# Softmax times values in three fp32r products instead of one fp32 product

## The chip, the cores and the metric

The kernel runs on one core of a Trainium2 chip. The metric is the time of one launch on the device in microseconds (us), median of several runs. The engines are called PE (matrix products), ACT (scalar engine), DVE (vector engine), POOL (general engine) and SP (which issues most DMAs).

## What is computed

One inference step of an encoder with two layers, for 1024 frames of a new stream and 8 running streams of 16 frames each; all 1152 columns go through the same weights (model width 1024). Layer 0 is a mixer of a state-space model and a gated delta rule, then a gated feed-forward net. Layer 1 is attention in a sliding window with grouped heads, then a gated feed-forward net. The change is in the attention over the new stream:

```
q: 16 heads, k and v: 4 heads, head width 64, chunks of 64 frames
scores = einsum('bnqkgd,bnskd->bnkgqs', q, kband) / 8   # chunk n sees chunks n-2, n-1, n
p = softmax over s of [scores, sink][..., :-1]
o = einsum('bnkgqs,bnskd->bnqkgd', p, vband)            # this product is changed
out = o @ wo
```

Everything is fp32 in the reference.

## The kernel before

Matrices are kept with features on the 128 partitions and frames in the free dimension, in three blocks of 384 columns. The large products with weights are not done in fp32, but as three products in fp32r, a rounded form of fp32: a matrix is split in a rounded part (`hi`, made by an ACT copy into an fp32r tile) and a remainder (`lo`, made by a DVE subtraction), and hi·hi + hi·lo + lo·hi is summed in PSUM. `gemm_block` and `project` do that; their PSUM tile is called pg in the profile.

`swa` is the attention of layer 1. It projects keys and values (`gemm` with `wkv`); values are transposed on PE so that frames stand on partitions, and stored in one fp32 tile `vT` of nine 128-frame tiles by 256 columns (4 heads of 64). Then, for each of two pairs of key/value heads, `qgemm(pair)` projects the queries and `attend(pair)` runs 16 chunks. `prompt_unit` does one chunk for the two heads e = 0, 1 of the pair:

- the scores of the four query heads that share a key head, two matmuls into a PSUM tile pS (L1896);
- `soft`: maximum, exponential, sum, reciprocal and scaling on DVE, ACT and POOL, in one of three tiles `pt_` (L1871 to L1884);
- up to two 128-frame key tiles hold the window. For each, two transposes on PE (L1916) into a PSUM tile pT (two banks), then a DVE copy of all of them to SBUF (L1919, or L1921 where there is one key tile);
- the product with the values: per key tile one fp32 matmul (L1923). The stationary operand is `vT[lo:hi, t, 64 columns of this head]`, the moving one the 256 columns of transposed weights, and the result stands on the 64 PSUM partitions of this head in one tile pO.

After both heads, pO is stored in one operation: an ACT copy to `o0` for the first pair (L1977), and for the second pair directly as the rounded part and remainder that the output projection wants (L1988, L1989). After every second chunk `sample_unit` does one of the running streams in the same way, in fp32, through the same tile ring `sT`.

Each engine has its own queue, in an order that is fixed before the run by a planner: it simulates the engines with costs of its own and, among what is ready in that simulation, takes what stands earliest in the program (a block `Sooner` moves work up). So `attend(0)` has precedence over `qgemm(1)`, which stands behind it, and `attend(1)` over the first half of the output projection (`project`, L1543 to L1545), whose first input, the first pair's output, is complete at that time. These projections are what PE does while it would wait for a softmax. When `attend(1)` is over, `between` closes the attention's pools and frees their space for the second half of the output projection.

`ssq` is a fixed tile in a pool of the whole program, which holds sums of squares for the norms and serves as scratch elsewhere; the attention does not use it.

Of the kernel before, what the change touches and what calls it, by code (L numbers as in the profile page):

```python
# [25 lines left out]
TP = 1024  # L26
# [176 lines left out]
def body(tc, nc, I, O):  # L203
# [136 lines left out]

    ssq = rp.tile([128, T], F32, name="ssq")

    def square_in(x, k, b, i, new, parts, keep=None):

        s = blk(b)
        if i == 0:
            S.activation(ssq[:, s], x[:, k, s], AF.Square)
            parts[:] = [ssq[:, s]]  # L350
            return
        both = keep is not None
        sq = keep if both and i == 2 else new()
        S.activation(sq, x[:, k, s], AF.Square)
        if i == KC - 1 or both and i == 2:
            parts.append(sq)
        elif both and i % 2 == 0:
            V.tensor_add(parts[1], parts[1], sq)
        else:
            P.tensor_add(ssq[:, s], ssq[:, s], sq)  # L360

    def rms(r, b, parts, first=0, banks=None):


        s = blk(b)
        y, v = r[:, s], ssq[:, s]
# [95 lines left out]
    def ffn(x, pre, l, w, nxt):  # L462
# [221 lines left out]
        for n in "gu":  # L684
# [4 lines left out]
        nt = rp.tile([128, BW], F32, name="nt", tag="nt", bufs=1)  # L689
        rooms = [[tp.tile([128, BW], F32, name=f"sg{i}") for i in range(2)] + [ssq[:, blk(b)] for b in range(NB)] + [nt] +  # L690
                 [r[:, blk(UP_T[t])] for t in (0, 2)],
# [78 lines left out]
        nt, rr = rp.tile([128, BW], F32, name="nt", tag="nt", bufs=1), new_r()  # L770
        sums = [nt, rr[:, blk(0)], ssq[:, blk(0)], ssq[:, blk(1)]] + sums + [ssq[:, blk(2)], rr[:, blk(1)], rr[:, blk(2)]]
        seven = {(n, m): sums[4 * i + m] for i, n in enumerate(("B11", "T2", "T3")) for m in range(4)}
# [282 lines left out]
    P.tensor_copy(PW[:, :, 0], L8)  # L1055
    tp = ssq[:, 0:256].rearrange("p (n q g) -> p n q g", q=2, g=16)
    for n in (1, 2, 4, 8):
# [30 lines left out]
    XG = XE[:, 0:TP // CS].rearrange("p (a c) q g -> p a c q g", c=16)  # L1088
    sc = ssq.rearrange("p (u v g) -> p u v g", v=2, g=16)
    for c in range(1, 16):  # L1090
# [200 lines left out]
    for hh in range(1, H):  # L1291
        gate_in(hh, ssq)

# [47 lines left out]
    def gate(t):  # L1341
        zs = h4(ssq[:, blk(t % 2, 512)])
        Q.dma_start(zs, d_z[:, :, blk(t, 128)].rearrange("h p i -> p h i"))
        return zs
# [465 lines left out]
def swa(env):  # L1810
# [6 lines left out]
    kT = qp.tile([128, 2, T], F32, name="kT")  # L1817
    vT = qp.tile([128, NT, 256], F32, name="vT")
    qt = [p_.tile([128, 4 * T], F32, name=f"q{i}") for i, p_ in enumerate((q0p, qp))]
# [7 lines left out]
    for t in (snk, snks):  # L1827
        V.tensor_scalar(t[:, 1], t[:, 0], -1.0, None, op0=ALU.mult)
    wk, c_wk = po.open("swv")

    W = [panel(I["wkv"][m]) for m in range(2)]
# [4 lines left out]
    for m in range(2):  # L1836
        def ev(b, s, p):
# [8 lines left out]
    Q.dma_start(O["pv"], vT[:, 7, :])  # L1846
# [4 lines left out]
    Q.dma_start(O["sv"][:, 112:128, :], vT[:, 8, :])  # L1851
    d_vn = env["dr"].tile([128, 256], F32, name="d_vn")
    Q.dma_start(d_vn, vT[:, 8, :])

# [9 lines left out]
    def small(n, w=2):  # L1864
        return wk.tile([128, w], F32, name=n, tag=n, bufs=4)

# [18 lines left out]

    def prompt_unit(pair, c, out):
        pO = mbank("pO")
        for e in range(2):
# [35 lines left out]
        out(c, pO[:, :256].rearrange("p (i k) -> p i k", i=4))  # L1924

    ns = npt

    def sample_unit(pair, b, out, ck, cvt, vn):
# [9 lines left out]
        pT = mbank("pT")  # L1938
        sT = wk.tile([128, 2, 2, 128], F32, name="sT", tag="sT", bufs=2)
        for i in range(2):  # L1940
            PE.transpose(pT[:, i * 128:i * 128 + 128], pt[:, 0, 64 + 128 * i:192 + 128 * i], ident)
        V.tensor_copy(sT[:, 0].rearrange("p a k -> p (a k)"), pT[:, :256])
        pO = mbank("pO")
        for e in range(2):
            hs = slice(64 * e, 64 * e + 64)
            PE.matmul(pO[hs, :64], cvt[:, b, hs], sT[:, 0, 0, hs], start=True, stop=False)
            PE.matmul(pO[hs, :64], vn[:, b, hs], sT[0:16, 0, 1, hs], start=False, stop=True)
        out(b, pO[:, :64].rearrange("p (i k) -> p i k", i=4))

# [11 lines left out]
    def attend(pair, store, then=lambda: None):  # L1961
# [5 lines left out]
        Q.dma_start(cvt, I["cv"][:, :, 128 * pair:128 * pair + 128].rearrange("b t c -> t b c"))  # L1967
        then()
        for c in range(16):
            prompt_unit(pair, c, lambda c, p: store(c, slice(0, 64), p))  # L1970
            if c % 2:
                continue
            b = c // 2
            sample_unit(pair, b, lambda b, p: store(16 + b // 4, slice(LS * (b % 4), LS * (b % 4) + LS), p), ck, cvt, vn)

    qgemm(0)
    attend(0, lambda c, k, src: S.copy(o0[:, c, :, k], src))  # L1977
    qgemm(1)
# [6 lines left out]

    def store1(c, k, src):
        oh, ol = (t[:, c % 6, :, k] for t in oT[c // 6][1])
        S.copy(oh, src)  # L1988
# [5 lines left out]

    def between():
        c_wk()
        c_qp()
# [15 lines left out]
```

## Time and profile before

| what | value |
|---|---|
| median of 3 runs | 2709.62 us (2709.35 to 2715.86) |
| profiled execution, its own time | 2709.62 us |
| its span, first to last instruction | 2707.8 us |
| mean granted TensorE clock | 0.973 |
| PE busy | 2556.9 us, 94% of the span |
| DVE, POOL, ACT busy | 1979.3, 1625.4, 1146.3 us |
| the two calls of `attend` | about 1550 to 1850 us |

The profile is one execution, recorded instruction by instruction. An fp32 matmul appears as two records on PE, an fp32r matmul as one (both are printed as f32). PEld is the load of the stationary operand. The recorded duration of a matmul runs from its start to its modelled end, and matmuls overlap in the pipeline: what one costs is read from the distance of the starts, or from the chain that ended last. The granted clock is a share of 2.4 GHz; 0.50 is 1.2 GHz.

### The profile page before, as it was taken

The page shows a single profiled execution, that of the slowest core. Times are in us where ns is not written, and L with a number is a line of the kernel's source. Part 1 is how long each engine was busy: PE and PEld are TensorE (multiplying, and loading weights), DVE is VectorE, ACT ScalarE, POOL GpSimd, SP SyncE. Part 2 cuts the span into 40 slices and gives each one's busy share as a digit, 9 for nine tenths or more (in the row PEclk, how much of TensorE's full clock was granted, in tenths as well). Part 3 has the DMA queues.
Part 4 walks back from the last instruction along what each step waited for, and adds up shares of the span by engine and source line. Part 5 has one row for each costly group of instructions (what it writes and reads, how often), then busy time and mean ns, then how long its engine had stood idle before and what let it go on. Part 6 is the DMA issues. An engine that isn't in the chain of part 4 may idle for free.

```text
span 2707.8 us, 40377 instructions
## 1 busy us (share of the span) xinstructions
PE 2556.9 (94%) x14777; PEld 2382.5 (88%) x14777; DVE 1979.3 (73%) x3235; ACT 1146.3 (42%) x2312; POOL 1625.4 (60%) x1659
## 2 busy tenths in 40 slices
PE   6898899999799999989999999999889999989996
PEld 5787798999799999989998977677889999989996
DVE  7847874567878777798866245555878777788967
ACT  5234465345544444443333134434544444444333
POOL 8749532125698888887532022213589888888735
PEclk9899999999999999999999999998999999999998
DMA  6432377633122222253213200202122222243311
GB/s 208 126 114 77 102 237 230 190 121 111 37 101 79 91 74 74 93 185 100 93 38 106 69 16 19 93 30 86 43 98 82 86 76 74 76 177 119 96 49 70
DMA packets 164166, 267.21 MB, mean 99 GB/s; under 512 B 34188, under 2 KB 123948, under 8 KB 162928
## 3 DMA queue, kind: packets, MB, share of 16 engines
q1 hardware_dynamic: 163392, 262.28, 29.9%
q8 instruction: 116, 1.90, 0.3%
q10 hardware_dynamic: 576, 2.36, 0.2%
q14 instruction: 82, 0.67, 0.1%
HBM read 186.92 MB, written 79.51 MB: 98 GB/s over the span
## 4 chain that ended last, share of the span: by engine, by line
PE 68%; POOL 11%; DVE 11%; DMA 4%; issue 4%; ACT 1%; SPq 1%; DVEq 0%; POOLq 0%; ACTq 0%
PE pa L455 7%; PE pa L454 7%; PE pa L453 7%; PE pd L455 3%; PE pd L453 3%; PE pd L454 3%; PE b L453 3%; PE b L455 3%; PE b L454 3%; PE pg L320 3%; PE pg L322 3%; PE pg L321 3%; PE pO L1923 2%; PE pg L1543 2%; PE pg L1544 2%
## 5 line engine op out<-in xcount | busy, mean ns | idle before, releaser
L453 PE MATMUL pa<-u,whi 128*128 128x384 f32 x904 | 307.4, 341 | 20.6 <-ACT whi L535 10.9
L454 PE MATMUL pa<-u,whi 128*128 128x384 f32 x904 | 306.3, 339 | 1.1 <-DVE u L269 1.1
L455 PE MATMUL pa<-u,wlo 128*128 128x384 f32 x904 | 298.1, 338 | 6.3 <-DVE wlo L536 6.3
L535 ACT CAST whi<-x 128x1024 fp32r<-128x1024 f32 (+2 forms) x184 | 132.5, 747 | 257.1 <-PE pa L454 172.1
L454 PE MATMUL pd<-g,whi 128*128 128x384 f32 x708 | 240.2, 339 | 0.0
L453 PE MATMUL pd<-g,whi 128*128 128x384 f32 x708 | 239.3, 338 | 0.0
L455 PE MATMUL pd<-g,wlo 128*128 128x384 f32 x708 | 237.8, 338 | 0.4 <-DVE wlo L298 0.4
L536 DVE TENSOR_TENSOR wlo<-x,whi 128x1024 fp32r<-128x1024 f32 (+2 forms) x184 | 213.0, 1180 | 24.7 <-ACT whi L535 24.4
L1884 POOL TENSOR_SCALAR p<-p,rd 128x192 f32<-128x192 f32 (+3 forms) x80 | 60.0, 752 | 278.4 <-DVE rd L1878 157.3
L453 PEld LDWEIGHTS pa<-u,whi 128*128 128x128 f32 x904 | 171.5, 190 | 25.5 <-ACT whi L535 14.5
L297 ACT CAST whi<-raw 128x1024 fp32r<-128x1024 f32 x113 | 116.6, 1049 | 173.7 <-PE pg L321 81.6
L531 POOL TENSOR_TENSOR x<-x 128x256 f32<-128x256 f32 (+1 forms) x186 | 169.4, 931 | 24.9 <-DVE wlo L536 18.8
L531 POOL TENSOR_TENSOR x<-raw 128x256 f32<-128x256 f32 (+1 forms) x186 | 169.4, 933 | 21.5 <-DVE wlo L536 13.3
L298 DVE TENSOR_TENSOR wlo<-raw,whi 128x1024 fp32r<-128x1024 f32 x113 | 165.3, 1465 | 22.7 <-ACT whi L297 20.3
L455 PEld LDWEIGHTS pa<-u,wlo 128*128 128x128 f32 x904 | 170.8, 190 | 7.7 <-DVE wlo L536 7.6
L531 POOL TENSOR_TENSOR cm<-raw 128x256 f32<-128x256 f32 (+1 forms) x150 | 144.3, 983 | 49.8 <-DVE wlo L536 18.5
L454 PEld LDWEIGHTS pa<-u,whi 128*128 128x128 f32 x904 | 171.8, 190 | 2.3 <-DVE u L269 1.9
L453 PE MATMUL pa<-u,x 128*128 128x384 f32 x428 | 145.8, 341 | 5.3 <-ACT x L535 2.8
L320 PE MATMUL pg<-h0h,whi 128*128 128x384 f32 x384 | 135.4, 353 | 12.1 <-DVE ut L970 11.4
L454 PE MATMUL pa<-u,x 128*128 128x384 f32 x428 | 144.9, 338 | 0.0
L455 PE MATMUL pa<-u,x 128*128 128x384 f32 x428 | 141.6, 339 | 0.0
L790 DVE TENSOR_TENSOR g<-gf,g 128x384 fp32r<-128x384 f32 x132 | 137.4, 1066 | 5.3 <-ACT g L789 5.3
(735 smaller groups left out, 8113.7 us busy)
## 6 DMA issues: line engine op xcount, KB each, us to landing
gf<-d_g SPq DMA_DIRECT2D x44, 576.0 KB
raw<-in_wd_dram SPq DMA_DIRECT2D x44, 512.0 KB
raw<-in_wg_dram SPq DMA_DIRECT2D x24, 512.0 KB
raw<-in_wu_dram SPq DMA_DIRECT2D x24, 512.0 KB
raw<-in_win_dram SPq DMA_DIRECT2D x21, 512.0 KB
x<-in_wg_dram SPq DMA_DIRECT2D x20, 512.0 KB
x<-in_wu_dram SPq DMA_DIRECT2D x20, 512.0 KB
d_r<-x SPq DMA_DIRECT2D x24, 384.0 KB
```

The source lines that it names most:

```text
L297: S.copy(hi, raw)
L298: V.tensor_sub(lo, raw, hi)
L320: PE.matmul(p[:, :BW], hi[:, c], rh, start=(i == 0), stop=False)
L321: PE.matmul(p[:, :BW], hi[:, c], rl, start=False, stop=False)
L322: PE.matmul(p[:, :BW], lo[:, c], rh, start=False, stop=(i == len(ks) - 1))
L453: PE.matmul(p, hi[:, c], uh, start=start, stop=False, skip_group_check=more)
L454: PE.matmul(p, hi[:, c], ul, start=False, stop=False, skip_group_check=more)
L455: PE.matmul(p, lo[:, c], uh, start=False, stop=stop, skip_group_check=more)
L531: (P.tensor_add if sg > 0 else P.tensor_sub)(cm[:, 256 * j:256 * (j + n)], fa, ga)
L535: S.copy(hi[:, c], src)
L536: V.tensor_sub(lo[:, c], src, hi[:, c])
L790: eng.tensor_sub(op[1], t, op[0])
```

## The change

Four things change, all for the product of the prompt chunks; `sample_unit` keeps its fp32 product.

1. The values are stored by pairs of heads, eight tiles of 128 frames by 128 columns, as a rounded part `vh` and a remainder `vl`. Those of the first pair are made when the values are transposed; the second pair's are kept in fp32 (`v1`) and split at the start of `attend(1)` by `values`, into the same buffers. `vl` lives in the buffer of `ssq`, which therefore becomes a tile that is made anew after the attention.
2. The transposed weights are rounded by an ACT copy out of PSUM (`sh`), and DVE subtracts that from PSUM for the remainder (`sl`); before, one DVE copy took them out.
3. Per key tile there are three fp32r matmuls with a stationary operand of 128 by 128 (both heads of the pair) and 256 moving columns; of the result only the 64 partitions of the head in question are used. Its two heads stand side by side in pO, 256 columns each.
4. The output is stored in two operations of 64 partitions, one for each head.

Beside that the ring of the small softmax vectors goes from 4 to 3 buffers, and the two value tiles that go out as results have a tile of their own.

```diff
+    V0 = halves()
+    v1 = qp.tile([128, NV, 128], F32, name="v1")
...
-            S.copy(vT[:, 3 * b:3 * b + 3, 128 * m:128 * m + 128], pt[:, :BW].rearrange("p (t i) -> p t i", t=3))
+            p3 = pt[:, :BW].rearrange("p (t i) -> p t i", t=3)
+            t = slice(3 * b, min(3 * b + 3, NV))
+            p2 = p3[:, :t.stop - t.start]
+            S.copy((v1 if m else V0[0])[:, t], p2)
+            if not m:
+                V.tensor_sub(V0[1][:, t], p2, V0[0][:, t])
+            if b == NB - 1:
+                S.copy(vT[:, :, 128 * m:128 * m + 128], p3[:, 1:])
...
-        return wk.tile([128, w], F32, name=n, tag=n, bufs=4)
+        return wk.tile([128, w], F32, name=n, tag=n, bufs=3)
...
+    def values(pair):
+        if not pair:
+            return V0
+        vh, vl = halves()
+        S.copy(vh, v1)
+        V.tensor_sub(vl, v1, vh)
+        return vh, vl
...
-            sT = wk.tile([128, 2, 2, 128], F32, name="sT", tag="sT", bufs=2)
+            sh, sl = (wk.tile([128, 512], F32R, name=n, tag=n, bufs=2) for n in ("sh", "sl"))
...
-            if nk == 2:
-                V.tensor_copy(sT.rearrange("p i a k -> p (i a k)"), pT)
-            else:
-                V.tensor_copy(sT[:, 0].rearrange("p a k -> p (a k)"), pT[:, :256])
-            for i, (t, w, lo, hi) in enumerate(ks):
-                PE.matmul(pO[hs, :256], vT[lo:hi, t, 64 * kv:64 * kv + 64], sT[lo:hi, i].rearrange("p a k -> p (a k)"), start=(i == 0), stop=(i == nk - 1))
-        out(c, pO[:, :256].rearrange("p (i k) -> p i k", i=4))
+            for o in (sh, sl):
+                a, b = o[:, :256 * nk], pT[:, :256 * nk]
+                S.copy(a, b) if o is sh else V.tensor_sub(a, b, sh[:, :256 * nk])
+
+            terms = [(x_, y[:, blk(i, 256)], t) for i, (t, *_) in enumerate(ks) for x_, y in ((v[0], sh), (v[0], sl), (v[1], sh))]
+            for i, (x_, y, t) in enumerate(terms):
+                PE.matmul(pO[:, blk(e, 256)], x_[:, t], y, start=(i == 0), stop=(i == len(terms) - 1))
+        for e in range(2):
+            hs = slice(64 * e, 64 * e + 64)
+            out(c, hs, pO[hs, blk(e, 256)].rearrange("p (i k) -> p i k", i=4))
...
+        v = values(pair)
         for c in range(16):
-            prompt_unit(pair, c, lambda c, p: store(c, slice(0, 64), p))
+            prompt_unit(pair, c, lambda c, hs, p: store(c, hs, slice(0, 64), p), v)
```

## Rows read from the trace of the kernel before

**Rows 1.** The page, part 1: busy time, share of the span, instructions.

```profile
PE 2556.9 (94%) x14777; PEld 2382.5 (88%) x14777; DVE 1979.3 (73%) x3235; ACT 1146.3 (42%) x2312; POOL 1625.4 (60%) x1659
```

**Rows 2.** Windows: stretch, its length, busy us (records) by engine, clock, DMA.

```profile
1450.00:1500.00 50.00, 50.00 (x288) 48.64 (x287) 17.78 (x32) 9.17 (x15) 0.46 (x1) 1.00 0.23 69
...
1675.00:1703.00 28.00, 27.89 (x159) 17.22 (x158) 17.25 (x63) 14.71 (x57) 6.68 (x9) 1.00 0.24 72
...
sum 300.00, PE 296.84 PEld 204.05 DVE 161.56 ACT 125.94 POOL 59.98; mean PE 59.37 PEld 40.81 DVE 32.31 ACT 25.19 POOL 12.00
```

**Rows 3.** The chain that ended last, 1550 to 1850 us, shares by line.

```profile
by line: PE pO L1923 22.4%; PE pS L1896 17.4%; PE pT L1916 10.6%; PE pg L320 6.5%; PE pg L322 6.4%; PE pg L1543 6.1%; PE pg L321 6.1%; PE pg L1545 5.8%; PE pg L1544 5.7%; PE pO L1946 2.8%; PE pO L1947 2.7%; PE pS L1933 2.2%; PE pT L1941 1.9
```

**Rows 4.** Windows of the tile pg alone: length, PE, PEld, DVE, ACT, clock, DMA.

```profile
1550.00:1675.00 125.00, 63.76 (x289) 48.75 (x289) 6.93 (x16) 0.00 (x0) 1.00 0.06 18
1675.00:1703.00 28.00, 5.19 (x26) 3.94 (x24) 0.62 (x2) 0.00 (x0) 1.00 0.24 72
1703.00:1716.00 13.00, 0.00 (x0) 0.00 (x0) 1.01 (x2) 0.00 (x0) 0.82 0.88 339
```

**Rows 5.** Windows of 4 us: PE, PEld, DVE, ACT, POOL, clock, DMA.

```profile
1714.00:1718.00 4.00, 4.00 (x12) 2.48 (x11) 2.41 (x9) 1.39 (x6) 0.60 (x1) 0.50 0.18 75
...
1844.00:1848.00 4.00, 3.15 (x8) 1.24 (x8) 0.76 (x2) 1.92 (x3) 0.41 (x1) 0.55 0.00 0
```

**Rows 6.** Windows of line L1923 alone: length, PE, PEld, clock, DMA.

```profile
1550.00:1675.00 125.00, 25.67 (x84) 7.96 (x84) 1.00 0.06 18
1675.00:1703.00 28.00, 9.76 (x35) 3.11 (x36) 1.00 0.24 72
1703.00:1716.00 13.00, 3.93 (x10) 0.97 (x10) 0.82 0.88 339
```

**Rows 7.** Timeline of PE: start, duration, line, operation, tiles, records.

```profile
1587.48 1.09 PE L1916 MATMUL pT<-ident,p 128*128 128x128 f32 x8
1588.33 0.42 PE L320 MATMUL pg<-h0h,whi 128*128 128x384 f32 x1
...
1604.09 0.44 PE L320 MATMUL pg<-h1h,whi 128*128 128x384 f32 x1
1604.37 0.34 PE L321 MATMUL pg<-h1l,whi 128*128 128x384 f32 x1
1604.54 0.35 PE L322 MATMUL pg<-h1h,wlo 128*128 128x384 f32 x1
```

**Rows 8.** Timeline of PE at half clock.

```profile
1717.72 0.52 PE L1544 MATMUL pg<-o0l,whi 128*128 128x384 f32 x1
1718.04 0.52 PE L1545 MATMUL pg<-o0h,wlo 128*128 128x384 f32 x1
```

**Rows 9.** Groups by form: busy us, mean ns, idle before and its releaser.

```profile
L1919 DVE COPY sT<-pT 128x512 f32<-128x512 f32 x56 | 38.6, 690 | 29.4 <-PE pT L1916 28.5
L1500 ACT COPY o<-pO 128x512 f32<-128x512 f32 x8 | 4.7, 585 | 15.3 <-PE pO L1499 15.3
L1359 DVE TENSOR_TENSOR pn<-pn,sq 128x512 f32<-128x512 f32 x9 | 6.3, 698 | 0.2
L1977 ACT COPY o<-pO 128x256 f32<-128x256 f32 x16 | 6.0, 373 | 30.3 <-PE pO L1923 30.3
L297 ACT CAST whi<-raw 128x1024 fp32r<-128x1024 f32 x11 | 11.4, 1043 | 14.1 <-PE pg L321 12.1 <-PE pg L1544 1.9
L298 DVE TENSOR_TENSOR wlo<-raw,whi 128x1024 fp32r<-128x1024 f32 x11 | 14.1, 1291 | 2.3 <-PE pO L1923 2.3
```

**Rows 10.** The chain that ended last, in order: start, length, what.

```profile
1827.26 1.15 PE pO L1923 x4
...
1830.67 0.84 PE pS L1896 x4
...
1844.28 2.10 PE pO L1923 x4
```

**Rows 11.** Waits in 1550 to 1850: in total, times, longest.

```profile
PE pO L1923 <- DVE sT L1919: 1.6, 2, 0.8
```

More of the change, by code (lines that the diff above doesn't have):

```diff
@@ L339, in split_in, with new_ssq @@
         V.scalar_tensor_tensor(h[b][k][1], x[:, k, blk(b)], wk, h[b][k][0], ALU.mult, ALU.subtract)
-    ssq = rp.tile([128, T], F32, name="ssq")
+    SS = []
+    def new_ssq():
+        SS[:] = [rp.tile([128, T], F32, name="ssq", tag="ssq", bufs=1)]
+    new_ssq()
     def square_in(x, k, b, i, new, parts, keep=None):
@@ L348, in square_in @@
         if i == 0:
-            S.activation(ssq[:, s], x[:, k, s], AF.Square)
-            parts[:] = [ssq[:, s]]
+            S.activation(SS[0][:, s], x[:, k, s], AF.Square)
+            parts[:] = [SS[0][:, s]]
             return
@@ L359, in square_in @@
         else:
-            P.tensor_add(ssq[:, s], ssq[:, s], sq)
+            P.tensor_add(SS[0][:, s], SS[0][:, s], sq)
     def rms(r, b, parts, first=0, banks=None):
         s = blk(b)
-        y, v = r[:, s], ssq[:, s]
+        y, v = r[:, s], SS[0][:, s]
         t = rp.tile([128, BW], F32, name="nt", tag="nt", bufs=1)
@@ L689, in ffn @@
         nt = rp.tile([128, BW], F32, name="nt", tag="nt", bufs=1)
-        rooms = [[tp.tile([128, BW], F32, name=f"sg{i}") for i in range(2)] + [ssq[:, blk(b)] for b in range(NB)] + [nt] +
+        rooms = [[tp.tile([128, BW], F32, name=f"sg{i}") for i in range(2)] + [SS[0][:, blk(b)] for b in range(NB)] + [nt] +
                  [r[:, blk(UP_T[t])] for t in (0, 2)],
@@ L770, in ffn @@
         nt, rr = rp.tile([128, BW], F32, name="nt", tag="nt", bufs=1), new_r()
-        sums = [nt, rr[:, blk(0)], ssq[:, blk(0)], ssq[:, blk(1)]] + sums + [ssq[:, blk(2)], rr[:, blk(1)], rr[:, blk(2)]]
+        sums = [nt, rr[:, blk(0)], SS[0][:, blk(0)], SS[0][:, blk(1)]] + sums + [SS[0][:, blk(2)], rr[:, blk(1)], rr[:, blk(2)]]
         seven = {(n, m): sums[4 * i + m] for i, n in enumerate(("B11", "T2", "T3")) for m in range(4)}
@@ L1055, in body @@
     P.tensor_copy(PW[:, :, 0], L8)
-    tp = ssq[:, 0:256].rearrange("p (n q g) -> p n q g", q=2, g=16)
+    tp = SS[0][:, 0:256].rearrange("p (n q g) -> p n q g", q=2, g=16)
     for n in (1, 2, 4, 8):
@@ L1088, in body @@
     XG = XE[:, 0:TP // CS].rearrange("p (a c) q g -> p a c q g", c=16)
-    sc = ssq.rearrange("p (u v g) -> p u v g", v=2, g=16)
+    sc = SS[0].rearrange("p (u v g) -> p u v g", v=2, g=16)
     for c in range(1, 16):
@@ L1291, in body @@
     for hh in range(1, H):
-        gate_in(hh, ssq)
+        gate_in(hh, SS[0])
     mphase(pX=1, pU=1, pc=1, pO=1, sm=1, m=1)
@@ L1341, in gate @@
     def gate(t):
-        zs = h4(ssq[:, blk(t % 2, 512)])
+        zs = h4(SS[0][:, blk(t % 2, 512)])
         Q.dma_start(zs, d_z[:, :, blk(t, 128)].rearrange("h p i -> p h i"))
@@ L1817, in swa, with halves @@
     kT = qp.tile([128, 2, T], F32, name="kT")
-    vT = qp.tile([128, NT, 256], F32, name="vT")
+    NV = TP // 128
+    def halves():
+        return (qp.tile([128, NV, 128], F32R, name="vh", tag="vh", bufs=1),
+                env["rp"].tile([128, T], F32, name="vl", tag="ssq", bufs=1)[:, :TP].bitcast(F32R).rearrange("p (t i) -> p t i", t=NV))
+    V0 = halves()
+    v1 = qp.tile([128, NV, 128], F32, name="v1")
     qt = [p_.tile([128, 4 * T], F32, name=f"q{i}") for i, p_ in enumerate((q0p, qp))]
@@ L1829, in swa @@
     wk, c_wk = po.open("swv")
+    vT = wk.tile([128, 2, 256], F32, name="vT")
     W = [panel(I["wkv"][m]) for m in range(2)]
@@ L1842, in ev @@
                 PE.transpose(pt[:, blk(t, 128)], vv[:, blk(t, 128)], ident)
[L1843 removed]
+            p3 = pt[:, :BW].rearrange("p (t i) -> p t i", t=3)
[6 more added lines that the diff above has]
+                S.copy(vT[:, :, 128 * m:128 * m + 128], p3[:, 1:])
         gemm(panel(I["wkv"][2 + m]), h, ev)
     Q.dma_start(O["pk"].rearrange("m p t -> p m t"), kT[:, :, TP - 128:TP])
[L1846 removed]
+    Q.dma_start(O["pv"], vT[:, 0, :])
     for m in range(2):
@@ L1850, in swa @@
     Q.dma_start(O["sv"][:, 0:112, :], I["cv"][:, 16:128, :])
-    Q.dma_start(O["sv"][:, 112:128, :], vT[:, 8, :])
+    Q.dma_start(O["sv"][:, 112:128, :], vT[:, 1, :])
     d_vn = env["dr"].tile([128, 256], F32, name="d_vn")
-    Q.dma_start(d_vn, vT[:, 8, :])
+    Q.dma_start(d_vn, vT[:, 1, :])
     c_wk()
@@ L1884, in soft, with prompt_unit @@
                 P.tensor_scalar(q, q, rd[:, a:a + 1], None, op0=ALU.mult)
-    def prompt_unit(pair, c, out):
+    def values(pair):
[5 more added lines that the diff above has]
+        return vh, vl
+    def prompt_unit(pair, c, out, v):
         pO = mbank("pO")
@@ L1938, in sample_unit @@
         pT = mbank("pT")
-        sT = wk.tile([128, 2, 2, 128], F32, name="sT", tag="sT", bufs=2)
+        sT = wk.tile([128, 2, 128], F32, name="sT", tag="sT", bufs=1)
         for i in range(2):
             PE.transpose(pT[:, i * 128:i * 128 + 128], pt[:, 0, 64 + 128 * i:192 + 128 * i], ident)
-        V.tensor_copy(sT[:, 0].rearrange("p a k -> p (a k)"), pT[:, :256])
+        V.tensor_copy(sT.rearrange("p a k -> p (a k)"), pT[:, :256])
         pO = mbank("pO")
@@ L1945, in sample_unit @@
             hs = slice(64 * e, 64 * e + 64)
-            PE.matmul(pO[hs, :64], cvt[:, b, hs], sT[:, 0, 0, hs], start=True, stop=False)
-            PE.matmul(pO[hs, :64], vn[:, b, hs], sT[0:16, 0, 1, hs], start=False, stop=True)
-        out(b, pO[:, :64].rearrange("p (i k) -> p i k", i=4))
+            PE.matmul(pO[hs, :64], cvt[:, b, hs], sT[:, 0, hs], start=True, stop=False)
+            PE.matmul(pO[hs, :64], vn[:, b, hs], sT[0:16, 1, hs], start=False, stop=True)
+        out(b, slice(0, 128), pO[:, :64].rearrange("p (i k) -> p i k", i=4))
     oT = [None, None]
@@ L1973, in attend @@
             b = c // 2
-            sample_unit(pair, b, lambda b, p: store(16 + b // 4, slice(LS * (b % 4), LS * (b % 4) + LS), p), ck, cvt, vn)
+            sample_unit(pair, b, lambda b, hs, p: store(16 + b // 4, hs, slice(LS * (b % 4), LS * (b % 4) + LS), p), ck, cvt, vn)
     qgemm(0)
-    attend(0, lambda c, k, src: S.copy(o0[:, c, :, k], src))
+    attend(0, lambda c, hs, k, src: S.copy(o0[hs, c, :, k], src))
     qgemm(1)
@@ L1984, in swa, with store1 @@
     c_q0()
-    def store1(c, k, src):
-        oh, ol = (t[:, c % 6, :, k] for t in oT[c // 6][1])
+    def store1(c, hs, k, src):
+        oh, ol = (t[hs, c % 6, :, k] for t in oT[c // 6][1])
         S.copy(oh, src)
@@ L1995, in between @@
     def between():
+        env["new_ssq"]()
         c_wk()
```

## The prediction

> **What bounds the kernel now.** I read the page first: PE is busy for 94% of the span, DVE for 73% [rows 1]. A share over 2.7 ms says little of one stage, so next came the windows around the changed lines. From 1550 to 1850 us, where both calls of `attend` run, PE is busy 297 of 300 us, DVE 162, ACT 126, POOL 60 [rows 2]. The reader is to see there that no other engine is above 54%. The chain inside that stretch gives L1923, the product that the change rewrites, 22.4%, some 67 us [rows 3].
>
> Third, what PE does when attention isn't ready: it runs projection blocks (tile pg), and these do not last. In 1550 to 1675 there are 289 of their records, in 1675 to 1703 only 26, in 1703 to 1716 none [rows 4]. So a pair has a filled stretch, in which a late softmax costs nothing, and an unfilled end, in which PE has nothing else. At the end of either pair the granted clock goes to half, 0.50 from 1714 to 1718 and 0.55 from 1844 to 1848, where PE is busy for 3.15 of 4 us [rows 5].
>
> **The change: the product itself.** There are 64 heads (2 pairs, 16 chunks, 2 heads); 56 read two key tiles, 8 one. Before, a key tile is one fp32 matmul, two records in the trace, 240 in all. The four of a head hold the chain for 1.15 us [rows 10], 0.575 for one tile. After, a head has 6 fp32r matmuls (3 for one tile) with a 128x128 stationary operand and 256 moving columns: 360 records. None such is in the trace; the nearest are the projection's fp32r matmuls with 384 columns, which start 0.17 apart at full clock (0.1735 by the 288 records that fill 50 us in the stage before [rows 2]) and 0.32 apart at half [rows 7, 8]. 0.32 us for 384 columns at half clock is 0.16 at full, so 0.0135 is left beside the streaming; for 256 columns 0.107 + 0.0135 = 0.12. A head then costs 0.72, and 56 x 0.43 + 8 x (0.575 - 0.36) = 25.8 us go. Bounds: a floor of 0.1735 whatever the columns gives 1.04 a head and 6.5 us; the fp32 transposes, full 128x128 loads with two passes over 128 columns, come every 0.106 (eight from 1587.48 to 1588.33) [rows 7], and that gives 0.64 a head and 30.9 us. I take 0.12, because rows at two clocks agree on it.
>
> **Its borders.** Going from a part-sized stationary operand to a full one costs about 0.1: the first projection record after L1896 takes 0.28 to the next one instead of 0.173 [rows 7]. L1923 is part-sized now (64 columns) and full after, but half its neighbours are L1896, which keeps its 64 rows. 64 x 0.05 = 3.2 us go, between 0 and 6.4. With the product that is 29.0 us of PE work, 0.45 a head.
>
> A rule speaks against the step from 64 to 128 stationary columns: the Trainium skill, TensorE: Matmul & The Clock Gate, section LDWEIGHTS, has a load take the number of columns over 1.2 GHz whatever the rows, so by that page one load goes from 53 to 107 ns. The transposes every 0.106, each record with a full load, show that here a full load lies under the matmul before it [rows 7]; by the row 25.8 us go, by the page's figures with nothing hidden a head would cost 6 x 214 ns = 1.28 us, more than now.
>
> **What is added on the way to the product.** Before, DVE copies the transposed weights (0.690 for 128x512). After, ACT rounds them out of PSUM and DVE subtracts. ACT's 128x512 PSUM copies take 0.585; DVE's 128x512 two-operand operation on PSUM takes 0.698, the length of the copy it replaces [rows 9]. So DVE stays, ACT gains 56 x 0.585 + 8 x 0.37 = 36 us, and the chain of a head is 0.6 us longer. The output is stored by halves: 32 more ACT copies of 0.37 (12 us) and 16 more DVE subtractions, at some 0.45, between that copy and the 0.698 (7 us) [rows 9]. ACT goes from 126 to some 175 of the stretch, DVE to some 170: neither is the bound where PE has other work. No DMA is added; the split of the values in the value projection adds three subtractions of some 0.55 and two copies, on engines that are busy for 17.8 and 9.2 of 50 us in that stage while PE is busy throughout [rows 2]; without that cover they would cost some 2 us. The smaller ring (`small` 4 to 3) bounds nothing that the three `pt_` tiles don't bound already; cost nothing, and if a softmax waited for it, it is part of the pace below.
>
> **What the unfilled ends give back.** In 1550 to 1675 there are 84 records of L1923, 23 heads (four with two records): 5.4 us a head; 289 x 0.1735 = 50 us of the 125 are projection [rows 4, 6]. If the softmax chain keeps that pace, 0.45 less attention on PE per head means that the 50 us are used up after 19.3 heads rather than 23, and 12.7 heads of a pair run without cover. The unfilled pace of before: 28 us less 26 x 0.1735, over 35 records (8.75 heads), 2.7 us a head [rows 4, 6]. PE alone would now need 2.25. ACT was busy 14.71 us there, 1.68 a head [rows 2]; plus 0.585 and 0.185 that is 2.45 before any waiting in its strict order, so 2.7 stays likely and I take it: the gain is lost on these heads, 2 x 12.7 x 0.45 = 11.4 us. Bounds: ACT without a gap, 2.45, loses 5; the worst pace seen, 10 records in the 13 us from 1703 to 1716, about 4.3 us a head [rows 6], loses 52. I stay near 2.7, since 4.3 was read at the turn, at a mean clock of 0.82.
>
> **The turn and the tail.** At the second pair `values` copies and subtracts 128x1024 (1.04 and 1.29 [rows 9]) into buffers that the first pair's products still read. It waits for the last of them; queued behind it on ACT are the next softmaxes and on DVE their maxima, and the second pair's first product waits for both. Before, that product followed within a few us. No projection record runs in those 13 us [rows 4], so nothing covers: 2.3 us, between 0 and 4.6 (all of it repeated at half clock). In the tail the last two heads add 0.6 of ACT each, and their products at half clock go from 2.10 [rows 10] to 6 x 0.227 = 1.4; the doubled store adds 0.8: 0.5 in all, between -1 and +2. The new `ssq` tile waits for the last product, but its first write comes after that in any case: nothing.
>
> **The sum.** -25.8 - 3.2 + 11.4 + 2.3 + 0.5 = -14.8 us. The profiled execution took 2709.62 us, of which the span is 2707.8; it is also the median of the three runs. Forecast 2694.8 us.
>
> **Rivals.** *Record floor.* If a full load or the issue sets 0.1735 a record, PE loses only 6.5 + 3.2 us; the give-back shrinks with it to some 3.5, and with 2.8 for turn and tail the time is about 2706. For it: no row has fewer than 384 fp32r columns at full clock. Against: the transposes at 0.106.
>
> *The load is not hidden.* L1896 shows what an exposed load costs: its four records of 192 columns hold the chain for 0.84 [rows 10], 0.21 each, 0.16 of it two passes of streaming, so 0.05; L1923's 0.2875 holds 0.075. With 0.12 + 0.075 a head costs 1.17, nothing is won on the product, and the time is 2709 to 2712. By the page named above it would be 1.28 a head and about 2717. The transposes speak against it.
>
> *The softmax chain takes over (slower).* The place is the unfilled end of each pair; the mechanism is ACT's strict order, where the new rounding waits for PE's transposes and holds up the next exponentials, so that two pT banks stay occupied longer and PE runs dry and drops to half clock [rows 5]. The break-even is (29.0 - 2.8) / 25.4 = 1.03 us above 2.25, a pace of 3.3 us a head. At the 4.3 seen at the turn: -29.0 + 52 + 2.8 = +26, 2735 us. For it: ACT and DVE already wait for each other there. Against: PE waited for the transposed weights only twice in 300 us, 1.6 us in all [rows 11], and the planner can put ready work in between.
>
> **How the numbers follow.** Faster or slower by over 0.3% is 8.1 us, about what a measurement of this kernel can tell: below 2701.5 and above 2717.7. The forecast's case, PE freed at about 0.12 a record and partly given back, has 0.71 (its own range 2677 to 2703: 30.9 + 6.4 with 5 given back at one end, a pace near 3 at the other; 0.01 of it falls to "same"). The floor 0.09 and the load 0.07 lie in "same". The chain has 0.13, from 2702 to 2735, of which 0.09 is slower and 0.04 the same. Faster 0.70, same 0.21, slower 0.09. The range reaches over the floor and the load: 2677 to 2712.
>
> **What would show it.** The product's records 0.12 apart on PE and their group near 0.72 us a head, stretch 1550 to 1850 shorter by 12 to 20 us, ACT 40 to 50 us busier there, pg records used up sooner, and new PE waits for the rounding or the subtraction at the two unfilled ends. Records at 0.1735 or 0.2 would make the first step wrong; a stretch not shorter in spite of 0.12 would show the chain; a stretch shorter by the full 29 would show that I gave back too much.

## The result, and the profile after

| kernel | median us | runs | ratio to the kernel before, 95% interval |
|---|---|---|---|
| before | 2709.62 | 5 (2707.51 to 2715.86) | 1 |
| after | 2678.2 | 5 (2675.01 to 2683.9) | 0.9877 [0.9861, 0.9892] |

The change makes the kernel 1.2% faster, some 31 to 33 us, where 14.8 were forecast. The direction and the range held; the size was wrong by a factor of two.

The profiled execution of after took 2678.2 us with a span of 2676.4 and a mean clock of 0.978. Part 1 of its page, which answers to [rows 1]:

```profile
span 2676.4 us, 40734 instructions
PE 2524.3 (94%) x14897; PEld 2403.3 (90%) x14897; DVE 1986.1 (74%) x3255; ACT 1187.3 (44%) x2411; POOL 1624.0 (61%) x1659
```

PE lost 32.6 us of busy time, ACT gained 41, DVE 7. The 120 more records on PE are the product's: 360 instead of 240.

First, how long the attention lasts, in windows of all engines (length, PE, PEld, DVE, ACT, POOL, clock, DMA). It now ends near 1823 instead of near 1850:

```profile
1551.40:1823.40 272.00, 267.45 (x1699) 227.82 (x1699) 169.66 (x572) 167.44 (x589) 59.07 (x80) 0.99 0.13 43
...
1824.00:1901.00 77.00, 70.67 (x386) 67.18 (x386) 57.80 (x96) 40.49 (x75) 41.36 (x35) 1.00 0.30 100
```

PE is idle for 272.00 - 267.45 = 4.6 us, against 3.2 in the 300 us of before [rows 2]: PE still sets the pace, although ACT is up from 126 to 167. The second row is the output projection and the norm behind the attention, at full clock throughout. The same stretch of the kernel before:

```profile
1850.00:1933.00 83.00, 76.66 (x389) 72.06 (x388) 58.61 (x96) 40.51 (x74) 41.69 (x35) 0.93 0.28 92
```

It does the same work (389 and 386 records), needs 6 us more, and has a clock of 0.93: 0.07 x 83 = 5.8 us are clock alone, in a stage whose work the change does not touch. The attention itself, from its first scores to the end of its last product, holds 553 projection records in either kernel, so what differs there on PE is the product, the waits and the clock.

Second, the turn between the pairs, 4 us at a time, after [rows 5]:

```profile
1696.00:1700.00 4.00, 3.43 (x22) 2.36 (x22) 3.48 (x11) 3.98 (x15) 1.19 (x2) 0.94 0.54 214
1700.00:1704.00 4.00, 2.61 (x14) 1.84 (x12) 3.14 (x16) 3.48 (x16) 0.97 (x2) 0.50 0.62 195
1704.00:1708.00 4.00, 4.00 (x21) 3.44 (x21) 3.20 (x10) 2.33 (x9) 1.22 (x2) 0.70 0.97 398
...
1820.00:1824.00 4.00, 3.56 (x23) 2.63 (x21) 2.69 (x5) 3.80 (x7) 0.32 (x1) 1.00 0.00 0
```

From 1550 to 1901 one stretch at half clock is left, from 1699.6 to 1706.4 by the granted clock. Before, from 1550 to 1933, there were four, 27 us together: at the turn (1711.3 to 1721.5), at the end of the second pair (1844.4 to 1854.6), and two behind it (1878.5 to 1881.9, 1929.7 to 1933.1). The end of the second pair, 0.55 in [rows 5], is now at 1.00.

Third, the projections that fill. Windows of the tile pg alone (length, PE, PEld, DVE, ACT, clock, DMA), after [rows 4], and then of the product's line, now L1956 (length, PE, PEld, clock, DMA), after [rows 6]:

```profile
1550.00:1667.00 117.00, 62.19 (x297) 49.92 (x295) 7.57 (x18) 0.00 (x0) 1.00 0.07 19
1667.00:1700.00 33.00, 4.90 (x24) 4.11 (x24) 0.00 (x0) 0.00 (x0) 0.99 0.36 122
```

```profile
1550.00:1667.00 117.00, 23.22 (x132) 18.97 (x132) 1.00 0.07 19
```

The filled stretch holds 132 records, 24 heads (the first four of a pair have three records, the others six). Before it held 23. So it ended 8 us sooner, at a pace of 4.9 us a head instead of 5.4, and not after fewer heads.

Fourth, the product itself. Timeline of PE after (start, duration, line, operation, tiles, shape):

```profile
1600.05 0.28 PE L1956 MATMUL pO<-sl,vh 128*128 128x256 f32 x1
1600.17 0.28 PE L1956 MATMUL pO<-sh,vl 128*128 128x256 f32 x1
1600.29 0.28 PE L1956 MATMUL pO<-sh,vh 128*128 128x256 f32 x1
1600.40 0.28 PE L1956 MATMUL pO<-sl,vh 128*128 128x256 f32 x1
```

The starts are 0.12 apart, as taken. In the chain that ended last, shares by line from 1550 to 1824, and pieces (start, length, what):

```profile
by line: PE pS L1928 17.5%; PE pO L1956 16.4%; PE pT L1948 10.3%; PE pg L320 7.0%; PE pg L321 6.7%; PE pg L322 6.7%; PE pg L1549 6.3%; PE pg L1551 6.0%; PE pg L1550 6.0%; PE pS L1968 2.8%; PE pO L1981 2.6%; PE pO L1982 2.6%; PE pT L1976 1.2
...
1694.07 1.06 ACT vh L1914
1695.15 1.23 DVE vl L1915
...
1710.93 0.91 PE pO L1956 x6
```

The product's share falls from 67 us [rows 3] to 0.164 x 274 = 45. A head holds the chain for 0.91 where it held 1.15 [rows 10]; 0.2 of the 0.91 lies beyond six spacings of 0.12. The two operations of `values` stand on the chain at the turn, 2.3 us as forecast, and the half clock follows them.

What ACT and DVE got, by form (busy us, mean ns, idle before and its releaser), and PE's waits for them from 1550 to 1824 (in total, times, longest):

```profile
L1952 DVE TENSOR_TENSOR sl<-pT,sh 128x512 fp32r<-128x512 f32 x56 | 38.4, 686 | 18.3 <-ACT sh L1952 17.7
...
L1952 ACT CAST sh<-pT 128x512 fp32r<-128x512 f32 x56 | 32.8, 585 | 14.0 <-PE pT L1948 11.8 <-PE pO L1956 1.8
...
L2025 DVE TENSOR_TENSOR o1l<-pO,o1h 64x256 fp32r<-64x256 f32 x30 | 12.6, 418 | 3.7 <-ACT o1h L2024 3.3
...
L2013 ACT COPY o<-pO 64x256 f32<-64x256 f32 x32 | 11.7, 365 | 11.6 <-PE pO L1956 11.4
```

```profile
PE pS L1928 <- ACT p L1899: 2.0, 2, 1.4
PE pO L1956 <- DVE sl L1952: 1.3, 2, 1.0
PE pT L1948 <- ACT p L1905: 0.6, 1, 0.6
PE pO L1956 <- ACT sh L1952: 0.5, 1, 0.5
```

The durations are close to those read from other operations before (585, 698, some 450 and 370). PE waits 4.4 us in all, 1.8 of them for the rounding and the subtraction; before it was 3.0 us in all, 1.6 for the copy [rows 11]. So little of the longer chain shows up as waits.

**A ledger for the experiments.** Span times mean granted clock is what the run would take with PE's clock always full, here "full-clock us"; the rest of the span is "lost to the clock". It is bookkeeping: time that is lost while PE only waits counts as lost too. Means over all runs with a clock on record (of the kernel before the 49 taken beside the experiments; one slow run, at a clock of 0.853, is left out; standard errors 0.4 and 0.7 for before, 0.4 to 3 for the others); the last column is the attention alone, in the one profiled execution, by its length and its stretches at half clock:

| kernel | full-clock us | lost to the clock | attention: full-clock us and lost |
|---|---|---|---|
| before | 2637.1 | 72.9 | 292.2 and 8.1 |
| after | 2615.4 | 61.6 | 268.5 and 3.4 |

By these means 21.7 us are work and waits and 11.3 the clock, a quantity for which the forecast had no term; that is more than half of its miss. The split is looser than the standard errors say. In the 1550 us ahead of the attention, where no experiment edits anything and the change only the making of the values, the 14 profiles of all kernels range from 1508.8 to 1514.9 us at full clock and from 32 to 46 us lost. The attention alone is the safer measure of an edit's work, though it comes from one execution each.

### The profile page after: what moved, and what is told of

Its sections match the earlier page's. It is cut to its first block, busy times and chain, and to the rows that moved or that the text cites. A ratio compares the mean times of both kernels' runs of the same rounds, so it can differ in the third digit from the quotient of the medians.

```text
span 2676.4 us, 40734 instructions
## 1 busy us (share of the span) xinstructions
PE 2524.3 (94%) x14897; PEld 2403.3 (90%) x14897; DVE 1986.1 (74%) x3255; ACT 1187.3 (44%) x2411; POOL 1624.0 (61%) x1659
## 4 chain that ended last, share of the span: by engine, by line
PE 69%; POOL 11%; DVE 10%; DMA 4%; issue 4%; ACT 2%; SPq 0%; DVEq 0%; POOLq 0%; ACTq 0%
PE pa L461 7%; PE pa L459 7%; PE pa L460 7%; PE pd L459 4%; PE pd L460 4%; PE pd L461 4%; PE pg L320 3%; PE b L459 3%; PE pg L322 3%; PE pg L321 3%; PE b L460 3%; PE b L461 3%; PE pg L1549 2%; PE pg L1550 2%; PE pg L1551 2%
## 5 line engine op out<-in xcount | busy, mean ns | idle before, releaser
L320 PE MATMUL pg<-h0h,whi 128*128 128x384 f32 x384 | 136.1, 354 | 12.3 <-DVE ut L976 11.4
```

Source lines behind the costliest of these rows:

```text
L320: PE.matmul(p[:, :BW], hi[:, c], rh, start=(i == 0), stop=False)
```

## The experiments

The theories: that the sum was right and the gain lost by the give-back was overrated (PE work that goes, goes in full); that the gain beyond the work is clock; and, for the parts, that the precision, the wider stationary operand, the turn or the longer chain is what moves the time. In the table, PE work is the number of records times the spacing (for e11_fullfp32 without and with the borders); the differences are to the kernel that was edited; the last column is the attention in the profiled execution, at full clock.

| run | edited | PE work | ratio to before [95%] | full-clock us | lost | attention |
|---|---|---|---|---|---|---|
| e1_four | after | +14.4 | 0.9889 [0.9872, 0.9905] | 2615.9 (+0.5) | 64.3 (+2.7) | 274.9 (+6.4) |
| e2_one | after | -28.8 | 0.9815 [0.9797, 0.9833] | 2574.5 (-40.9) | 85.8 (+24.2) | 233.1 (-35.4) |
| e3_longer | after | 0 | 0.9934 [0.9916, 0.9952] | 2615.7 (+0.3) | 78.1 (+16.5) | 273.7 (+5.2) |
| e4_chain | before | 0 | 1.0023 [1.0014, 1.0033] | 2636.9 (-0.2) | 80.0 (+7.1) | 292.1 (-0.1) |
| e5_bytile | after | 0 | 0.9874 [0.9857, 0.9891] | 2606.1 (-9.3) | 70.1 (+8.5) | 266.2 (-2.3) |
| e6_half | after | 0 | 0.9859 [0.9839, 0.9879] | 2605.2 (-10.2) | 67.4 (+5.8) | 262.1 (-6.4) |
| e7_longer_four | e3_longer | +14.4 | 0.9932 [0.9914, 0.9949] | 2627.3 (+11.6) | 64.6 (-13.5) | 282.9 (+9.2) |
| e8_dense | before | +8.8 | 1.0024 [1.0012, 1.0036] | 2644.6 (+7.5) | 71.8 (-1.1) | 297.0 (+4.8) |
| e9_onetile | before | -32 | 0.9870 [0.9854, 0.9887] | 2602.7 (-34.4) | 72.2 (-0.7) | 257.4 (-34.8) |
| e10_half_bytile | e6_half | 0 | 0.9861 [0.9847, 0.9876] | 2607.3 (+2.1) | 65.5 (-1.9) | 262.2 (+0.1) |
| e11_fullfp32 | before | -17 to -20 | 0.9919 [0.9905, 0.9933] | 2617.3 (-19.8) | 69.3 (-3.6) | 274.8 (-17.4) |
| e12_half_four | e6_half | +14.4 | 0.9897 [0.9881, 0.9913] | 2615.9 (+10.7) | 64.9 (-2.5) | 273.3 (+11.2) |

### Less and more PE work

**A fourth product.**

```diff
-for x_, y in ((v[0], sh), (v[0], sl), (v[1], sh))]
+for x_, y in ((v[0], sh), (v[0], sl), (v[1], sh), (v[1], sl))]
```

> The changed kernel with a fourth product per key tile (remainder times remainder): two more fp32r records a head with two key tiles, one more with one, 120 records of 0.12 us = 14.4 us more PE work, nothing else changed. The changed kernel stands at 0.9877 of the kernel before (about -33 us). PE-bound theory (the planner keeps PE fed, the stretch is the sum of PE's work): +14 us, so about 0.993. Chain theory (the heads' pace is set by softmax, as my step on the give-back had it): PE has room, +0 to 6 us, 0.988 to 0.990.

Measured 2681.63 us, ratio 0.9889, as the chain theory has it: 14.4 us of work more, some 3 us of time, and 0.5 at full clock. Taken alone it would speak for a give-back of nearly everything. But the attention of its profile is 6.4 us longer at full clock, so the rest of the program, which was not edited, took back most of them; and the same edit on two neighbours (e7_longer_four, e12_half_four) costs 11.6 and 10.7 at full clock. So this is not the rule.

**One product of three** (the two correction products are left out).

```diff
-for x_, y in ((v[0], sh), (v[0], sl), (v[1], sh))]
+for x_, y in ((v[0], sh),)]
```

> The changed kernel with the first of the three products only (this leaves out the two correction products; rounding and subtraction are still made): 240 records fewer, 28.8 us less PE work. PE-bound theory: another -26 to -29 us, about 0.977. Chain theory: the heads can't come faster, so most of it is lost as waits: -0 to -10 us, 0.984 to 0.988.

Measured 2663.79 us, ratio 0.9815, between the two theories. At full clock more goes than the 28.8 us of work, and more than half of that comes back as clock: the profile has 24 us at half clock from 1680.0 to 1703.9 and 20 from 1792.7 to 1813.2, where the projections are used up.

**The kernel before with half of its product** (the second key tile's contribution is left out).

```diff
-for i, (t, w, lo, hi) in enumerate(ks):
-    PE.matmul(..., start=(i == 0), stop=(i == nk - 1))
+for i, (t, w, lo, hi) in enumerate(ks[:1]):
+    PE.matmul(..., start=(i == 0), stop=True)
```

> The kernel before with the fp32 product of the first key tile only (this leaves out the second key tile's product of 56 heads; everything else is still done): 56 x 0.575 = 32 us less PE work and 0.575 us less per head behind the transposed weights, no longer chain on ACT or DVE. In the kernel before, projection records last for 125 us and 23 heads, 5.4 us a head; in the changed kernel for 116 us and 23.5 heads, 4.9 a head. Theory A, the step as I predicted it (the softmax chain sets the pace of the heads, the product is no link of it): the pace stays at 5.4 a head, the projections are used up after some 18 heads, the unfilled ends grow from 20 to some 35 us each and the lost clock with them: 0.991 to 0.995. Theory B (the product is a link of the chain, so a shorter product raises the pace and the projections last for as many heads): pace 4.8 to 5.0, 22 heads or more, ends not longer, lost clock not above before: 0.987 to 0.989.

Measured 2676.1 us, ratio 0.987. This is the plainest test of the failed step, since the edit takes away nothing but PE work: no ACT copy, no fp32r, no turn. All 32 us go. The window of its product's line in the filled stretch (length, PE, PEld, clock, DMA):

```profile
1549.00:1659.00 110.00, 13.53 (x42) 3.98 (x42) 1.00 0.07 20
```

42 records are 21 heads: 5.2 us a head, where the forecast's reasoning has 5.4 whatever PE does. Both lie between the two theories (18 heads at 5.4, or 22 and more at 4.8 to 5.0); the time is that of theory B. In the attention of its profile 34.8 us go at full clock, though 27 us stand at half clock there, against 16 before.

**More PE work in the kernel before:** transposes of chunks 11 to 15, in which the projections run out, made twice.

```diff
-for a in range(2):
+for a in (0, 1, 0, 1) if c > 10 else (0, 1):
     PE.transpose(...)
```

> The kernel before with the transposes of the last five chunks of each pair made twice (same values): 20 heads x 0.44 = 8.8 us more of full-sized PE work, where the ends are unfilled and 13.6 us were lost to half clock (attention and what follows). Theory 'clock': it is held up, 1.000 or less, lost clock under 8 us. Theory 'sum of work': +9 us, 1.003, lost clock as before.

Measured 2717.51 us: +7.5 at full clock for 8.8 of work, clock -1.1. More records at the unfilled end are paid for and don't raise the clock by an amount that these runs can tell from nothing.

### A longer chain

**An ACT pass over the transposed weights** ahead of their copy, in after and in before:

```diff
+S.copy(pT[:, :256 * nk], pT[:, :256 * nk])
 for o in (sh, sl):
```

> The changed kernel with one more ACT pass over the transposed weights in PSUM (in place, no value changes): 0.585 us more in the chain of each head and 36 us more of ACT, no PE work. PE-bound theory: the chain has slack, +0 to 4 us, 0.988 to 0.989. Chain theory: 12.7 unfilled heads of each pair at 0.6 us, +15 us, 0.993, and more ACT waits in front of PE.

> The kernel before with the same ACT pass in place ahead of the DVE copy: the longer chain of the change without its product. PE-bound theory: +0 to 3 us, 0.999 to 1.001. Chain theory: 8 to 9 unfilled heads of each pair at 0.6 us, +10 us, 1.004.

Measured 2693.55 and 2718.9 us; the first is the time of the chain theory, the second lies between the two. But the cost is not the waits of that theory. In both it is clock, +16.5 and +7.1, and the full-clock time stands still to 0.3 us; in the attention alone it is +5.2 (in a profile that took 2702.25 us, the slowest of six runs) and -0.1. The windows show how that looks. After with the pass (length, PE, PEld, DVE, ACT, POOL, clock, DMA):

```profile
1695.00:1711.00 16.00, 15.86 (x69) 12.91 (x70) 7.35 (x29) 11.36 (x41) 2.91 (x5) 0.52 0.50 185
1711.00:1727.00 16.00, 14.77 (x57) 11.57 (x57) 10.70 (x39) 11.83 (x42) 3.68 (x6) 0.52 0.40 149
```

Before with the pass:

```profile
1836.00:1848.00 12.00, 12.00 (x30) 4.87 (x28) 4.50 (x17) 4.26 (x16) 2.56 (x4) 0.50 0.00 0
1848.00:1860.00 12.00, 12.00 (x38) 7.50 (x38) 5.54 (x7) 5.61 (x11) 3.29 (x2) 0.51 0.14 36
```

PE is "busy" for 15.86 of 16 and 12.00 of 12 us and still at half clock, and the table of waits shows less than the cost: 9.9 us instead of after's 4.4 in the attention of e3_longer, 2.9 instead of 3.0 in that of e4_chain. The Trainium skill, Perfetto Trace Analysis, section Identifying the Most-Contended Engine, says that the busy share of matmuls is not a good measure of how close a kernel is to its roofline, because pipelined instructions look smaller in the trace. These rows agree with the first half, with 100% at 0.50; none tests the reason.

**The pass and the fourth product together.**

> The changed kernel with both the additional ACT pass in the chain (alone: 0.9934, 17 us lost to half clock in the attention) and the fourth product (14.4 us of PE work; alone 0.9889). Theory 'clock': what the longer chain cost was half clock at the unfilled ends; more full-sized PE work there keeps the clock up, so the fourth product costs nothing on top or less: 0.988 to 0.993, lost clock well under 17 us. Theory 'sum of work and waits': both add, 0.995 to 0.999.

Measured 2694.61, against 2693.55 with the pass alone: no difference. +11.6 of work, -13.5 of clock. The time is that of the clock theory. Here more PE work went with a higher clock, which it didn't in e8_dense, e12_half_four and e1_four (-1.1, -2.5, +2.7).

### The parts of the change

**The turn.** The second pair's values are split tile by tile into the first pair's tiles, each as soon as the products that read that tile are through, instead of all at once:

```diff
-vh, vl = halves()
-S.copy(vh, v1)
-V.tensor_sub(vl, v1, vh)
+vh, vl = V0
+for t in range(NV):
+    S.copy(vh[:, t], v1[:, t])
+    V.tensor_sub(vl[:, t], v1[:, t], vh[:, t])
```

> The changed kernel with the second pair's values split tile by tile into the same two tiles, so that each of the eight pieces waits only for the first pair's reads of that piece instead of for all of them. In the profile of the changed kernel the two operations stand on the chain for 2.3 us at the turn, with 6.8 us at half clock behind them. If the turn costs what stands there: -2 to -5 us against the changed kernel (0.986 to 0.987). If something else is late there anyway: 0.988.

> The changed kernel with 64 stationary columns a head (alone 0.9859) and the second pair's values split tile by tile (alone 0.9874): no wait for all of the first pair's products at the turn. If both are worth what they showed: 0.984 to 0.986, ahead of the changed kernel (0.9877) by a little. If they are the planner's order and chance: 0.987 to 0.989.

Measured 2677.19 on after, and 2674.58 on e6_half: nothing that these runs can tell from no change. On after, 9.3 us at full clock go and 8.5 come back as clock; in the attention it is 2.3 us at full clock, what stood on after's chain, and the rest lies where nothing was edited. On e6_half neither moves. So the 2.3 us are real in after, but taking them off doesn't show in the time.

**64 stationary columns in fp32r,** one head instead of both, everything else as in after:

```diff
-PE.matmul(pO[:, blk(e, 256)], x_[:, t], y, ...)
+PE.matmul(pO[0:64, blk(e, 256)], x_[:, t, hs], y, ...)
...
-out(c, hs, pO[hs, blk(e, 256)]...)
+out(c, hs, pO[0:64, blk(e, 256)]...)
```

> The changed kernel with the 64 columns of one head as stationary operand of its fp32r products instead of both heads' 128 (both results on partitions 0 to 63, the store moves the second head's to 64 to 127). If a part-sized operand exposes its load and has borders (0.075 a record by the fp32 rows of before): 360 x 0.075 + 3 = +30 us, 0.999, and more time at half clock. If it is hidden as the full one: same as the changed kernel, 0.988.

Measured 2673.95, 0.9859 against 0.9877 for after, the intervals overlapping: the second head in the stationary operand buys nothing in fp32r. If anything the smaller operand is ahead: the attention of its profile is 6.4 us shorter at full clock. Timeline of PE:

```profile
1600.00 0.28 PE L1956 MATMUL pO<-sh,vh 128*64 128x256 f32 x1
1600.12 0.28 PE L1956 MATMUL pO<-sl,vh 128*64 128x256 f32 x1
1600.24 0.28 PE L1956 MATMUL pO<-sh,vl 128*64 128x256 f32 x1
```

0.12 again. The Trainium skill, TensorE: Matmul & The Clock Gate, section LDWEIGHTS, has a load last in proportion to its columns, so half as long here. The recorded loads are shorter, 134 ns instead of 188 in the filled stretch, though not by half; the spacing of the records does not move, which is what a load that lies under the matmul before it looks like.

**With a fourth product on that:**

> The kernel with 64 stationary columns a head (0.9859) and the fourth product: 14.4 us more PE work. In the changed kernel the fourth product cost only some 3 us (0.9889), 12 us in the kernel with the longer chain. If PE's work counts one to one and the first was the planner's order: +10 to 15 us, 0.990 to 0.991. If there is room on PE: +0 to 5, 0.986 to 0.988.

Measured 2680.92, ratio 0.9897: +10.7 at full clock for 14.4 of work, time +7, nearest to PE's work counting one to one.

**Both heads as one stationary operand, in fp32,** with no rounding, no remainder and no split values:

```diff
-PE.matmul(pO[hs, :256], vT[lo:hi, t, 64 * kv:64 * kv + 64], sT[lo:hi, i]..., ...)
+PE.matmul(pO[:, blk(e, 256)], vT[:, t, 128 * pair:128 * pair + 128], sT[:, i]..., ...)
```

> The kernel before with one part of the change alone: both heads of the pair as one 128x128 stationary operand and the stores by halves, the product still one fp32 matmul per key tile, no rounding. A record then should cost 0.213 to 0.22 (two passes over 256 columns at full clock, the load hidden as for the transposes) instead of 0.2875: four a head 0.87, 56 x 0.28 + 8 x 0.14 = 17 us less PE work, no longer chain. What it tells apart is the clock, of which the fp32r kernels with some 50 us without projections lost 2 to 7 us in and after the attention and the fp32 kernels 10 to 19. If part-sized operands are what loses it: lost clock like the changed kernel's, time 0.990. If the fp32 form is what loses it: as before, 0.993 to 0.994.

The edit also takes all 128 rows of a key tile, where half of the matmuls of before have 64, and stores by halves. Measured 2688.04, ratio 0.9919: this part alone brings two thirds of the gain, 19.8 us at full clock. The time lies between what the two theories on the clock have (0.990, and 0.993 to 0.994) and decides neither. Timeline of PE:

```profile
1604.18 1.03 PE L1923 MATMUL pO<-sT,vT 128*128 128x256 f32 x4
1605.05 0.38 PE L1943 MATMUL pT<-ident,p 128*128 128x128 f32 x2
...
1616.64 1.03 PE L1923 MATMUL pO<-sT,vT 128*128 128x256 f32 x4
1617.60 0.60 PE L1896 MATMUL pS<-kT,q 64*128 64x192 f32 x4
```

Four records of a head take 0.87 in front of a transpose, 0.217 each, and 0.96 here in front of scores (1.06 in the median of eleven such groups), where the same records with 64 columns took 1.15. By the starts in the trace of before, records with 64 columns are 0.267 apart within a matmul, with 128 rows and with 64 alike, and 0.31 where a matmul with the other number of rows, a transpose or scores follow. With 128 columns they are 0.216 apart. So the columns carry most of the difference between 1.15 and 0.87, and the change of rows the rest. In fp32 it is the full-sized operand that pays; in fp32r, with 128 rows throughout, 128 columns instead of 64 do not.

## Why the prediction was wrong in size

**The product, -25.8, and its borders, -3.2: right in sum.** The spacing is 0.12, the records' number is right, and the rivals that stood on it fall: a floor of 0.1735 a record and an exposed load are both refuted by the rows at 1600. What a head gains is best read where PE has no gap, from the first scores to the last product of the first pair's 24th head. All engines (before, after), and then the tile pg alone, there and on the eight heads that follow:

```profile
1550.00:1676.10 126.10, 126.10 (x693) 90.55 (x693) 64.07 (x224) 52.21 (x205) 25.55 (x33) 1.00 0.06 18
...
1551.40:1666.50 115.10, 115.10 (x737) 99.83 (x737) 62.92 (x221) 65.76 (x236) 25.16 (x33) 1.00 0.07 19
```

```profile
1550.00:1676.10 126.10, 64.13 (x290) 48.80 (x289) 7.55 (x18) 0.00 (x0) 1.00 0.06 18
1676.10:1703.20 27.10, 4.82 (x23) 3.89 (x23) 0.00 (x0) 0.00 (x0) 1.00 0.26 77
...
1551.40:1666.50 115.10, 60.79 (x289) 48.77 (x288) 7.57 (x18) 0.00 (x0) 1.00 0.07 19
1666.50:1693.90 27.40, 4.90 (x24) 4.11 (x24) 0.00 (x0) 0.00 (x0) 1.00 0.28 84
```

With the same projection work 24 heads take 11.0 us less, 0.46 a head, where the forecast has 0.45. The division between the two terms is less sure. By the starts, a group of six products is 0.81 ahead of the next record (median of 18 such groups), and not near 0.72 as the prediction wanted to see it; the step from a projection record to the first product record went from 0.27 to 0.17 (medians at full clock), so there the border that the prediction priced at 0.1 is gone.

**"What the unfilled ends give back", +11.4: this is the step that failed.** It let the pace of a filled head stay at 5.4 us, the pace of the softmax chain, so that the projections would be used up after 19.3 heads instead of 23. The pace went to 4.9 and the projections lasted for 24 heads. The stretches without a projection record at the ends of the pairs are 45 us long in after and 51 before, not longer. What was wrong is the reading of 5.4: it is not the pace of ACT and DVE, with PE filling what they leave; PE sets it, and the projections lie in it in proportion. e9_onetile shows it without the rest of the change: 32 us less product work, full-clock time 34.4 shorter, in the attention 34.8.

On a few heads the forecast's reasoning did hold. The first pair's last eight heads take 27.1 us before and 27.4 after, with 23 and 24 projection records (rows above): 8 x 0.45 = 3.6 us of PE work went there and nothing was won. PE was busy for 26.98 of the 27.1 us, so even a full share of busy time did not make the pace PE's. The second pair's last eight took 27.7 and 27.4 at full clock, but with 24 and 40 projection records, so most of the gain is there. In all the attention is 28.4 us shorter: 25.1 less PE work, 4.7 less half clock, 1.4 more waits. Against the 29.0 that is some 4 us of work given back, and 1.4 of waits, not 11.4. The prediction had named the sign: a stretch shorter by the full 29 would show that it gave back too much.

Over the runs that change PE work alone, e8, e9, e7 (on e3) and e12 (on e6) show 74 to 108% of it at full clock; e1 shows 3% and e2 142%, so any one kernel is uncertain by 12 to 14 us. In the attention alone all six lie between 44 and 123%.

**The turn and the tail, +2.3 and +0.5: the turn seen, but not decisive.** The two operations stand on the chain as worked out, and e5 takes 2.3 us off the attention at full clock; e5 and e10 show that their removal does not show in the time. No run tests the tail; the half clock that its products were priced at is gone from the second pair's end (1.00 from 1820 to 1824).

**No term for the clock.** The prediction read half clock at both ends [rows 5] and priced what happens there at the clock of before. In the means the clock is 11.3 of the 33 us; in the profiled pair 13, of which 4.7 lie in the attention and between 5 and 6 just behind it. The longer chain, with +0.6 us a head, has a price in just this coin (e3: 16.5 for another such pass), so the change may pay here too; it still comes out ahead.

At full clock the forecast would have been -14.8, against -21.7 over the whole kernel and -23.7 in the attention; without the give-back, -26.2. The rest is clock. That the range held is in part luck: its lower end, 2677, was made of faster records, wider borders and 5 us given back, and the time came near it by 4 to 5 given back and 11 us of clock.

**What stays open.** Why after has more clock than before is not settled. Less PE work doesn't do it (e9: -0.7), more at the end doesn't (e8: -1.1), the full-sized fp32 operand does a little (e11: -3.6), and the fp32r kernels without the extra pass lie between 61.6 and 70.1 (e2 aside), after being the lowest. Its three nearest relatives, e5, e6 and e10, have 8 to 10 us less at full clock and 4 to 8.5 more lost, at the same time: by them the change is -30 to -32 of work and -3 to -7 of clock. The total is firm and its split is not; in the attention alone the three have 2.3 to 6.4 less at full clock. The order of instructions is fixed anew by the planner for each kernel, and differences of some 10 us between relatives are its likely source; that was not tested, since no run held the order fixed.

No version beats after clearly: e6_half and e10_half_bytile are 0.2% ahead, within the intervals.

## What to carry to other kernels

Where PE is busy without a gap and is filled from a second source of work, as on the first 24 heads here, a pace per item is PE's pace: take PE work off and the pace falls, and a give-back needs evidence that another engine has no gap left. Where the filling has run out, a busy share of 99% is no such evidence. Price a longer dependency chain at the unfilled end in clock and not only in waits, and list the stretches at half clock with their lengths, including those behind the edited stage. Before splitting an fp32 product into rounded parts, try the full-sized stationary operand alone: here that was two thirds of the gain for none of the extra operations.

## What was not expected of the hardware

- In fp32, four records with a 64-column stationary operand take 1.15 us (half of them with 64 rows) and with a 128-column one 0.87, at the same 256 moving columns; a record with 128 rows and 64 columns is 0.267 from the next of its matmul, one with 128 columns 0.216. In fp32r 64 and 128 columns are the same, 0.12 a record.
- PE busy 12.00 of 12 us at a granted clock of 0.50 (e4_chain): a busy engine by the records, and a halved clock.
- An ACT pass of some 0.6 us a head cost nothing at full clock over the whole kernel (0.3 us) and 16.5 or 7.1 us in clock.
